# A fifth buffer for retention's values, and the last step of the group norm on ScalarE

## The chip, the cores and the metric

The kernel runs on one core of a Trainium2 chip. A core has a matrix engine (TensorE, PE in the profile; its weight loads are PEld), a vector engine (VectorE, DVE), a scalar engine (ScalarE, ACT), a general engine (GpSimd, POOL) and DMA queues (most of them started by SyncE, SP). The engines run side by side, each takes its own instructions in a fixed order, and they wait for one another through semaphores. The metric is the time of one execution in microseconds on the device.

## The reference, cut to what matters

The kernel computes one layer of a hybrid encoder: 1024 positions and 16 learned meta tokens, width 1024, float32. One projection of the normed input feeds retention (4 heads, keys of 128, values of 256), windowed attention and several gates. The change lies in retention and in the group norm behind it:

```python
    s = jnp.einsum("bnihd,bnjhd->bnhij", q, k) * decay[None, None]
    inner = jnp.einsum("bnhij,bnjhv->bnihv", s, v)
    ...
    kv = jnp.einsum("bnjhd,bnjhv->bnhdv", k * k_decay[None, None, :, :, None], v)
    ...
    cross = jnp.einsum("bnihd,bnhdv->bnihv", q * q_decay[None, None, :, :, None], s_prev)
    return (inner + cross).reshape(B, L, H, DV)
```

This is done forward and backward over blocks of 128 positions and summed. Then each head's 256 values of a position are normed:

```python
    mu = jnp.mean(o_r, axis=-1, keepdims=True)
    var = jnp.mean(jnp.square(o_r - mu), axis=-1, keepdims=True)
    o_r = ((o_r - mu) * lax.rsqrt(var + EPS)).reshape(B, T, RET_V)
```

## The kernel before

Every float32 product is made of three matmuls on halves: a value is split into a high part (a rounded copy) and a low part (the rest), and `mm3` (lines 71 to 76) multiplies high by high, low by high and high by low. The high part is a copy on ScalarE or GpSimd, the low part a subtraction on VectorE (`dve_lo`, line 89).

Retention runs for about the first 340 us, one head after another. The meta tokens are block 0 (16 rows), and the 1024 positions are blocks 1 to 8 of 128 rows. For one head, `retention` does this:

- `stage1(c)` (line 462) projects the values of block c (`projT`, tile `pv`, 24 matmuls of 256 columns; 16 for block 0) into one of the three PSUM banks `pj`. ScalarE copies the high part to `vh` (line 467) and VectorE makes the low part `vl`. For block 0 the values pass through `vmeta` first. Then it transposes the block's keys and multiplies keys and queries (tile `tr`, lines 470 and 472, in one of the two PSUM banks `p1`), scales the keys with the decays (`khf`, `khb` on ScalarE, line 480; low parts on VectorE, line 481) and makes the decayed scores (`sd`, `sh`, `sl`, lines 489 to 491).
- `stage2(c)` (line 502) uses them: the inner and the cross part (`pa`, in the one bank `p3`), which become the output `op` of the block (lines 510 and 511), and the products of keys and values (`pkv`), from which the forward state follows (`Sf`, its halves made by GpSimd and VectorE). The backward products are kept as `kvb` (line 527).
- After all blocks, the loop at line 576 goes backward from block 8 to 1: it updates the backward state, adds its part to the output (`pb`, lines 588 and 589), takes mean and variance of the block (lines 593 and 594), adds the epsilon (line 595, the instruction is kept as `near`) and raises it to the power -0.5 on GpSimd (line 596). The norm itself is kept as a function and run one step later, behind the next block's `near` (lines 600 and 601): a subtraction and a multiplication on VectorE (line 597). Two steps later `finish` transposes the block (tile `to`, line 565, again in `p1`), ScalarE scales it into `ost` (line 570), and SyncE stores it.
- The last two blocks of a head are finished during the next head (`pend`, lines 536 to 538).

In the backward loop, `fill(KT)` offers other work to TensorE: the next head's keys and queries (`gen_qk`), and parts of later stages. For head 3 it is the attention's first projections.

The text's order is not the order on an engine. A planner (`schedule_with_timeline_sim=True`) puts each engine's instructions in order when the kernel is built, by their place in the text and by times that it models itself, and instructions that are ready may overtake others. `tc.issue_after(i)` adds an edge: what is traced under it comes after `i` on `i`'s engine. The order is then fixed. How far a later step can be drawn ahead is limited by buffers: with `bufs=4`, the fifth block's `vh` can be written only when the first block's `vh` has been read for the last time, by `pkv` or `pa` in `stage2`.

Of the kernel before, what the change touches and what calls it, by code (L numbers as in the profile page):

```python
# [7 lines left out]
F32 = mybir.dt.float32  # L8
R = mybir.dt.float32r
AF = mybir.ActivationFunctionType  # L10
ALU = mybir.AluOpType
# [3 lines left out]
NM = 16  # L15
T = NM + SEQ
P = 128
# [21 lines left out]
def block_kernel(ctx: ExitStack, tc: tile.TileContext, xT, x, meta, w_in, w_rb, w_ab, w_out, vecs, dec, sink,  # L39
                 post_w, rope, tab, out):  # L40
    nc = tc.nc
# [29 lines left out]
    def mm3(o, ah, al, bh, bl, first, last, free_group=False):  # L71
        kw = {"skip_group_check": True} if free_group else {}
        nc.tensor.matmul(o, ah, bh, start=first, stop=False, **kw)  # L73
        nc.tensor.matmul(o, al, bh, start=False, stop=False, **kw)  # L74
        latest[:] = [nc.tensor.matmul(o, ah, bl, start=False, stop=last, **kw).ins]  # L75
        return latest[0]
# [11 lines left out]
    def dve_lo(o, i, hi):  # L88
        return nc.vector.tensor_tensor(o, i, hi.bitcast(F32), ALU.subtract).ins  # L89
# [65 lines left out]
    def projT(w, c, name, mt=None):  # L155
        wh, wl = w
        a, b = cols(c)
        t = pj(name)
        if c == 0:
            for k in range(KT):  # L160
                nc.tensor.matmul(t[0:48, 0:256], xm[:, k, 0:48], wh(k, 0, 256), start=k == 0, stop=False,
                                 skip_group_check=True)
                nc.tensor.matmul(t[0:NM, 0:256], xm[:, k, 0:NM], wl(k, 0, 256), start=False, stop=k == KT - 1,
                                 skip_group_check=True)
            nc.scalar.copy(mt, t[32:32 + NM, 0:256])
            nc.vector.tensor_tensor(mt, t[0:NM, 0:256], mt, ALU.add)
            return mt
        for k in range(KT):
            mm3(t[0:b - a, 0:256], xh[k][:, a:b], xl[k][:, a:b], wh(k, 0, 256), wl(k, 0, 256), k == 0, k == KT - 1)
        return t  # L170
# [88 lines left out]
    with tc.tile_pool(name="setup", bufs=1, reuse_waits="tile") as st:  # L259
# [57 lines left out]
        for k in range(KT):  # L317
            t = xr[k]
            parts = [(0, 528), (528, T)] if k == 0 else [(0, T)]
            for a, b in parts:  # L320
                high = nc.scalar.activation(xh[k][:, a:b], t[:, a:b], AF.Copy, scale=vec[:, k:k + 1]).ins
                with tc.issue_after(done) if done is not None and k > 2 else ExitStack():
                    low = nc.vector.scalar_tensor_tensor(xl[k][:, a:b], t[:, a:b], vec[:, k:k + 1],
                                                         xh[k][:, a:b].bitcast(F32), op0=ALU.mult,
                                                         op1=ALU.subtract).ins
# [17 lines left out]
        for c in range(9):  # L343
            a, b = cols(c)
            t = st.tile([P, D if c < 7 else T], F32, tag="xn" if c < 7 else "xr", bufs=7 if c < 7 else KT,
                        name=f"xn{c}")[:, 0:D]
# [46 lines left out]
    def kd_(i, c, n):  # L393
        return kdr[0:n, i, c:c + 1]
# [4 lines left out]
    def qdb(h, c):  # L399
        return qd[:, NH + h, c - 1:c]  # L400
# [4 lines left out]
    def cdb(h):  # L405
        return dtab[:, 24 + h:25 + h]
# [10 lines left out]
    rp = r_stack.enter_context(tc.tile_pool(name="rp", bufs=1, reuse_waits="tile"))  # L417
# [18 lines left out]
    def retention(h, fill):  # L436
# [7 lines left out]
        wv = wv0 if h == 0 else load_w(w_in, U_V + h)  # L444
        kvb = [None] + [rp.tile([P, 256], F32, tag="kvb", bufs=NB - 1, name=f"kvb{h}_{c}") for c in range(1, NB)]
        op = [rp.tile([P, 256], F32, tag="op", bufs=NB, name=f"op{h}_{c}") for c in range(NB)]
        vmeta = rp.tile([NM, 256], F32, tag="vmeta", bufs=2, name=f"vmeta{h}")
        st1 = {}
        state = {"f": None, "b": None}
        pins = []  # L450

        def qs(ts, c):
            return ts[(c - 1) // 4][:, P * ((c - 1) % 4):P * ((c - 1) % 4) + P]

        def ksl(c):
            if c == 0:
                return kt[:, 0, 0:NM]
            i = (c - 1) // 2
            o = P * ((c - 1) % 2) + (NM if i == 0 else 0)
            return kt[:, i, o:o + P]  # L460

        def stage1(c):
            n = NM if c == 0 else P
            pv = first.pop(0) if first else projT(wv, c, f"pv{h}_{c}", vmeta)
            vh = rp.tile([P, 256], R, tag="vh", bufs=4, name=f"vh{h}_{c}")
            vl = rp.tile([P, 256], R, tag="vl", bufs=4, name=f"vl{h}_{c}")
            state["v"] = nc.scalar.copy(vh[0:n], pv[0:n, 0:256]).ins
            state["vl"] = dve_lo(vl[0:n], pv[0:n, 0:256], vh[0:n])
            tr = p1(f"tr{h}_{c}")
            nc.tensor.transpose(tr[0:n, 0:P], ksl(c), ident)  # L470
            if c > 0:
                nc.tensor.matmul(tr[:, P:2 * P], ksl(c), qs(q, c), start=True, stop=True)
            kd = {}
            for d in ("f", "b"):
                if d == "f" and c > 7 or d == "b" and c < 2:
                    continue
                sc = kd_(h, c, n) if d == "f" else kd_(NH + h, c, n)
                a = rp.tile([P, P], R, tag="kh" + d, bufs=2, name=f"kh{d}{h}_{c}")
                b = rp.tile([P, P], R, tag="kl" + d, bufs=2, name=f"kl{d}{h}_{c}")
                nc.scalar.activation(a[0:n], tr[0:n, 0:P], AF.Copy, scale=sc)  # L480
                nc.vector.scalar_tensor_tensor(b[0:n], tr[0:n, 0:P], sc, a[0:n].bitcast(F32), op0=ALU.mult,
                                               op1=ALU.subtract)
                kd[d] = (a, b)
            s = None
            if c > 0:
                sd = rp.tile([P, P], F32, tag="sd", bufs=3, name=f"sd{h}_{c}")
                a = rp.tile([P, P], R, tag="sh", bufs=3, name=f"sh{h}_{c}")
                b = rp.tile([P, P], R, tag="sl", bufs=3, name=f"sl{h}_{c}")
                nc.vector.scalar_tensor_tensor(sd, tr[:, P:2 * P], r2[:, c:c + 1], DT[:, h], op0=ALU.mult, op1=ALU.mult)
                nc.scalar.copy(a, sd)  # L490
                dve_lo(b, sd, a)
                s = (a, b)
            st1[c] = (n, vh, vl, kd, s)

        def split_state(sr_, nm):
            a = rp.tile([P, 256], R, tag="Sh", bufs=2, name=f"Sh{nm}")
            b = rp.tile([P, 256], R, tag="Sl", bufs=2, name=f"Sl{nm}")
            state["S"] = pool_hi(a, sr_)
            dve_lo(b, sr_, a)
            return a, b  # L500
# [60 lines left out]
        def finish(c):  # L561
            o = op[c - 1]
            to = p1(f"to{h}_{c}")
            for e_ in range(2):
                nc.tensor.transpose(to[:, P * e_:P * e_ + P], o[:, P * e_:P * e_ + P], ident)  # L565
            if c % 2 == 0:
                ost[0] = rp.tile([P, 2, 256], F32, tag="ost", bufs=2, name=f"ost{h}_{c}")
            w0 = P * ((c - 1) % 2)
            for e_ in range(2):
                nc.scalar.activation(ost[0][:, e_, w0:w0 + P], to[:, P * e_:P * e_ + P], AF.Copy,  # L570
                                     scale=rnw[:, 2 * h + e_:2 * h + e_ + 1])
            if c % 2 == 1:
                nc.sync.dma_start(
                    oTr_d[2 * h:2 * h + 2, :, P * (c - 1):P * (c + 1)].rearrange("e p t -> p e t"), ost[0])

        for c in range(NB, 0, -1):
            o = op[c - 1]
            if c > 1:
                nxt = kvb[c - 1]
                if c < NB:  # L580
                    nxt = rp.tile([P, 256], F32, tag="S", bufs=2, name=f"Sb{h}_{c}")
                    nc.vector.scalar_tensor_tensor(nxt, state["b"], cdb(h), kvb[c - 1], op0=ALU.mult, op1=ALU.add)
                state["b"] = nxt
                state["bs", c - 1] = split_state(nxt, f"b{h}_{c}")
            if c < NB:
                bh, bl = state["bs", c]
                pb = p3(f"pb{h}_{c}")
                last["pb"] = mm3(pb[:, 0:256], qs(qh, c), qs(ql, c), bh, bl, True, True)
                nc.vector.scalar_tensor_tensor(o, pb[:, 0:256], qdb(h, c), o, op0=ALU.mult, op1=ALU.add)
            bs = rp.tile([P, 6], F32, tag="bs", bufs=2, name=f"bs{h}_{c}")  # L590
            mv = rp.tile([P, 2], F32, tag="mv", bufs=2, name=f"mv{h}_{c}")
            rs = rp.tile([P, 1], F32, tag="rs", bufs=2, name=f"rs{h}_{c}")
            nc.vector.bn_stats(bs, o)
            nc.vector.bn_aggr(mv, bs)
            near = nc.vector.tensor_scalar(rs, mv[:, 1:2], EPS, None, op0=ALU.add).ins
            nc.gpsimd.tensor_tensor(rs, rs, mhalf[:, 0:1], ALU.pow)
            state["n", c] = lambda o=o, mv=mv, rs=rs: nc.vector.tensor_scalar(o, o, mv[:, 0:1], rs, op0=ALU.subtract,
                                                                              op1=ALU.mult)
            if c < NB:
                with tc.issue_after(near):  # L600
                    state["n", c + 1]()
            if c < 8:
                with ExitStack() as behind:
                    for p in pins:
                        behind.enter_context(tc.issue_after(p))
                    fill(KT)
            if c < NB - 1:
                finish(c + 2)
# [958 lines left out]
```

## Time and profile before

| what | value |
|---|---|
| median of three runs | 1073.84 us (1072.59 to 1073.89) |
| profiled execution | 1072.16 us |
| its span (first to last instruction) | 1070.4 us |
| DMA | 179.46 MB, 168 GB/s on average |

The span is shorter than the execution's time, since something lies ahead of the first and behind the last instruction. In the profile's rows, a group has a line, an engine, an operation and the tiles it writes and reads (`out<-in`), its count, its busy time, the mean duration of one, and the idle time of the engine before it with what ended it. Buffer numbers are left out of tile names, so that all blocks' `pv` are one group. A matmul's duration overlaps with that of the next.

### The profile page before, as it was taken

The page shows a single profiled execution, that of the slowest core. Times are in us where ns is not written, and L with a number is a line of the kernel's source. Part 1 is how long each engine was busy: PE and PEld are TensorE (multiplying, and loading weights), DVE is VectorE, ACT ScalarE, POOL GpSimd, SP SyncE. Part 2 cuts the span into 40 slices and gives each one's busy share as a digit, 9 for nine tenths or more (in the row PEclk, how much of TensorE's full clock was granted, in tenths as well). Part 3 has the DMA queues.
Part 4 walks back from the last instruction along what each step waited for, and adds up shares of the span by engine and source line. Part 5 has one row for each costly group of instructions (what it writes and reads, how often), then busy time and mean ns, then how long its engine had stood idle before and what let it go on. Part 6 is the DMA issues. An engine that isn't in the chain of part 4 may idle for free.

```text
span 1070.4 us, 17180 instructions
## 1 busy us (share of the span) xinstructions
PE 1053.5 (98%) x5921; PEld 910.0 (85%) x5921; DVE 872.2 (81%) x1795; ACT 511.1 (48%) x1135; POOL 203.0 (19%) x268
## 2 busy tenths in 40 slices
PE   8999999999999999999999999999999999999997
PEld 7998999989989888988888888887888888787886
DVE  6887778869976887788868988999799799767765
ACT  5531432513413566665577644455456546333432
POOL 2434225143332222232210000000000000110032
PEclk9999999999999999999999999999999999999999
DMA  9321102113121253444357779899934756779363
GB/s 336 158 70 60 60 21 69 61 51 99 50 79 60 70 177 129 129 148 157 131 165 264 250 235 336 267 361 348 363 121 161 239 176 221 237 205 332 112 118 80
DMA packets 89337, 179.46 MB, mean 168 GB/s; under 512 B 9056, under 2 KB 31072, under 8 KB 88432
## 3 DMA queue, kind: packets, MB, share of 16 engines
q1 hardware_dynamic: 85360, 171.77, 47.1%
q0 software_dynamic: 3456, 6.29, 3.9%
q8 instruction: 47, 0.77, 0.3%
q14 instruction: 42, 0.34, 0.1%
q10 hardware_dynamic: 432, 0.28, 0.1%
HBM read 123.78 MB, written 57.67 MB: 170 GB/s over the span
## 4 chain that ended last, share of the span: by engine, by line
PE 85%; DVE 7%; ACT 3%; DMA 2%; issue 2%; SPq 0%; DVEq 0%; POOLq 0%; ACTq 0%
PE bz L74 8%; PE bz L73 8%; PE bz L75 8%; PE pv L75 3%; PE pv L73 3%; PE pv L74 3%; PE br L74 2%; PE br L75 2%; PE br L73 2%; PE bo L74 2%; PE bo L73 2%; PE bo L75 2%; PE ba L74 2%; PE ba L73 2%; PE ba L75 2%
## 5 line engine op out<-in xcount | busy, mean ns | idle before, releaser
L1184 POOL DMA_DIRECT2D mx_d<-c1a x4 | 3.7, 917 | 401.5 <-DVE c1a L1175 401.5
L74 PE MATMUL bz<-T,llz 128*128 128x512 f32 x192 | 75.8, 395 | 0.0
L75 PE MATMUL bz<-T,lhz 128*128 128x512 f32 x192 | 75.6, 395 | 0.0
L73 PE MATMUL bz<-T,lhz 128*128 128x512 f32 x192 | 75.2, 394 | 0.0
L74 PE MATMUL pv<-wh,big 128*128 128x256 f32 x256 | 73.0, 285 | 0.0
L75 PE MATMUL pv<-wl,big 128*128 128x256 f32 x256 | 72.5, 283 | 0.0
L73 PE MATMUL pv<-wh,big 128*128 128x256 f32 x256 | 72.4, 283 | 0.0
L74 PE MATMUL bz<-big,llz 128*128 128x512 f32 x176 | 69.7, 396 | 0.0
L75 PE MATMUL bz<-big,lhz 128*128 128x512 f32 x176 | 69.3, 394 | 0.0
L73 PE MATMUL bz<-big,lhz 128*128 128x512 f32 x176 | 68.9, 394 | 0.0
L1329 ACT ACTIVATE p<-raw,nm 128x401 f32<-128x401 f32 (+1 forms) x64 | 38.4, 602 | 43.5 <-DVE nm L1326 43.4
L74 PE MATMUL paq<-big,wl 128*128 128x512 f32 x128 | 50.8, 397 | 1.0 <-DVE wl L89 1.0
L73 PE MATMUL paq<-big,wh 128*128 128x512 f32 x128 | 51.8, 404 | 0.0
L75 PE MATMUL paq<-big,wh 128*128 128x512 f32 x128 | 50.4, 394 | 0.0
L1339 POOL TENSOR_SCALAR p<-p,den 128x400 f32<-128x400 f32 (+1 forms) x60 | 33.8, 576 | 83.1 <-DVE den L1332 73.7
L75 PEld LDWEIGHTS pv<-wl,big 128*128 128x128 f32 x256 | 48.3, 189 | 0.1
L73 PEld LDWEIGHTS pv<-wh,big 128*128 128x128 f32 x256 | 48.2, 188 | 0.2
L74 PEld LDWEIGHTS pv<-wh,big 128*128 128x128 f32 x256 | 48.2, 188 | 0.0
L74 PEld LDWEIGHTS bz<-T,llz 128*128 128x128 f32 x192 | 36.2, 188 | 8.6 <-DVE llz L89 0.2
L73 PEld LDWEIGHTS bz<-T,lhz 128*128 128x128 f32 x192 | 36.2, 188 | 8.4
L75 PEld LDWEIGHTS bz<-T,lhz 128*128 128x128 f32 x192 | 36.2, 188 | 8.4
L570 ACT ACTIVATE ost<-to,rnw 128x128 f32<-128x128 f32 x64 | 20.1, 365 | 47.7 <-PE to L565 40.5
(622 smaller groups left out, 3631.2 us busy)
## 6 DMA issues: line engine op xcount, KB each, us to landing
wrz<-in_w_in_dram SPq DMA_DIRECT2D x32, 512.0 KB, 6.1
wr<-in_w_in_dram SPq DMA_DIRECT2D x29, 512.0 KB, 3.6
e<-e SPq DMA_DIRECT2D x40, 256.0 KB, 4.0
we<-in_w_in_dram SPq DMA_DIRECT2D x16, 512.0 KB, 3.9
tg<-tg_d SPq DMA_DIRECT2D x32, 256.0 KB, 4.9
T<-preT SPq DMA_DIRECT2D x6, 1024.0 KB, 7.3
xn<-in_x_dram SPq DMA_DIRECT2D x8, 512.0 KB, 8.6
oTr_d<-ost SPq DMA_DIRECT2D x16, 256.0 KB, 2.1
```

Source lines behind the costliest of these rows:

```text
L73: nc.tensor.matmul(o, ah, bh, start=first, stop=False, **kw)
L74: nc.tensor.matmul(o, al, bh, start=False, stop=False, **kw)
L75: latest[:] = [nc.tensor.matmul(o, ah, bl, start=False, stop=last, **kw).ins]
L570: nc.scalar.activation(ost[0][:, e_, w0:w0 + P], to[:, P * e_:P * e_ + P], AF.Copy, scale=rnw[:, 2 * h + e_:2 * h + e_ + 1])
L1184: nc.gpsimd.dma_start(d, to, accum_op=ALU.add)
L1329: last["exp"] = nc.scalar.activation(p[:, 0:1 + wid], raw[e_][:, 0:1 + wid], AF.Exp, scale=-1.0, bias=nm_[:, e_:e_ + 1], accum_out=den[:, ...
L1339: nc.gpsimd.tensor_scalar(pt[e_][:, 0:wid], pt[e_][:, 0:wid], den[:, e_:e_ + 1], 1.0, op0=ALU.mult, op1=ALU.mult)
```

## The change

Three edits are in `retention`. The tiles `vh` and `vl` have five buffers in place of four. `vmeta` has one in place of two. The last step of the norm, (o - mean) rs with rs = (variance + epsilon)^-0.5, is computed as o rs + (-mean rs): VectorE makes the one-column product -mean rs in the place of the mean, and ScalarE applies it as an activation with a scale and a bias column. Both are traced where VectorE's subtraction stood, behind `near`; `issue_after` orders only the VectorE product, as `near` is on VectorE.

```diff
-        vmeta = rp.tile([NM, 256], F32, tag="vmeta", bufs=2, name=f"vmeta{h}")
+        vmeta = rp.tile([NM, 256], F32, tag="vmeta", bufs=1, name=f"vmeta{h}")
...
-            vh = rp.tile([P, 256], R, tag="vh", bufs=4, name=f"vh{h}_{c}")
-            vl = rp.tile([P, 256], R, tag="vl", bufs=4, name=f"vl{h}_{c}")
+            vh = rp.tile([P, 256], R, tag="vh", bufs=5, name=f"vh{h}_{c}")
+            vl = rp.tile([P, 256], R, tag="vl", bufs=5, name=f"vl{h}_{c}")
...
-            state["n", c] = lambda o=o, mv=mv, rs=rs: nc.vector.tensor_scalar(o, o, mv[:, 0:1], rs, op0=ALU.subtract,
-                                                                              op1=ALU.mult)
+
+            def norm(o=o, mv=mv, rs=rs):
+
+                nc.vector.scalar_tensor_tensor(mv[:, 0:1], mv[:, 0:1], -1.0, rs, op0=ALU.mult, op1=ALU.mult)
+                nc.scalar.activation(o, o, AF.Identity, scale=rs, bias=mv[:, 0:1])
+            state["n", c] = norm
```

## The prediction

> **What bounds the kernel now.** I read the page first, then busy time by stage, then the order on TensorE and ScalarE around one head change.
>
> ```profile
> span 1070.4 us, 17180 instructions
> PE 1053.5 (98%) x5921; PEld 910.0 (85%) x5921; DVE 872.2 (81%) x1795; ACT 511.1 (48%) x1135; POOL 203.0 (19%) x268
> PEclk9999999999999999999999999999999999999999
> PE 85%; DVE 7%; ACT 3%; DMA 2%; issue 2%; SPq 0%; DVEq 0%; POOLq 0%; ACTq 0%
> ```
>
> TensorE (PE) is busy for 98% of the span, at full clock, and makes 85% of the chain that ended last. The change leaves its 5921 matmuls as they are. So it can gain only where TensorE stands still or thins out, and lose only where it opens a new hole. The table of windows for retention (about 40 to 340 us) shows where it thins out. Its columns are the window, its length, then busy time and instructions of PE, PEld, DVE, ACT and POOL, clock, DMA share, GB/s.
>
> ```profile
> 40.00:340.00 300.00, 298.20 (x2238) 281.96 (x2238) 244.12 (x617) 99.29 (x296) 103.73 (x145) 1.00 0.18 58
> 95.00:117.00 22.00, 22.00 (x189) 21.84 (x188) 19.12 (x52) 6.04 (x19) 9.66 (x15) 1.00 0.23 76
> 117.00:122.00 5.00, 4.24 (x27) 3.13 (x26) 4.37 (x15) 2.77 (x10) 1.70 (x3) 1.00 0.16 52
> 122.00:127.00 5.00, 5.00 (x43) 4.85 (x42) 3.83 (x13) 2.76 (x10) 1.12 (x2) 1.00 0.17 56
> 187.00:192.00 5.00, 5.00 (x41) 4.59 (x40) 4.76 (x16) 3.04 (x10) 1.59 (x4) 1.00 0.17 56
> 258.00:265.00 7.00, 6.36 (x45) 5.25 (x44) 6.46 (x21) 3.77 (x13) 2.26 (x4) 1.00 0.23 76
> 273.00:283.00 10.00, 9.61 (x78) 9.21 (x77) 9.83 (x28) 4.42 (x17) 3.15 (x4) 1.00 0.32 107
> ```
>
> Matmuls overlap, so a busy PE hides holes; I count instructions. In a dense stretch 189 matmuls take 22 us, 0.1164 us each, or 43 in 5 us. From head 0 to head 1 (117 to 122) only 27 start: 16 short, 1.86 us. From 1 to 2 (187 to 192) 41: 0.23 us. From 2 to 3 (258 to 265) 45 where 60.1 fit: 1.76 us. These three sum to 3.85 us. In 273 to 283, inside head 3, there are 78 where 86 fit: 0.93 us at most, and 0.39 us idle at least; DVE is busy 9.83 of 10 us there.
>
> [...] By matmul busy all retention would have 1.80 us to give; by weight loads the three changes lack 1.87, 0.41 and 1.75 us, 4.03 us. [...]
>
> What opens the hole at 117 us, in TensorE's order (start, duration, instruction):
>
> ```profile
> 117.39 0.38 PE L565 MATMUL to<-ident,op 128*128 128x128 f32 x2
> 117.61 0.27 PE L470 MATMUL tr<-ident,kr 128*16 128x128 f32 x1
> 118.48 0.33 PE L470 MATMUL tr<-ident,kr 128*128 128x128 f32 x1 [0.61 <-ACT ost L570]
> 118.97 0.91 PE L73 MATMUL pkv<-vh,khf 16*128 16x256 f32 x2
> 119.81 0.38 PE L74 MATMUL pkv<-vh,klf 16*128 16x256 f32 x1
> 121.66 0.28 PE L73 MATMUL pv<-wh,big 128*128 128x256 f32 x1
> ```
>
> And ScalarE's copies of the values (`vh`, line 467):
>
> ```profile
> 107.25 0.37 ACT L467 CAST vh<-pv 128x256 fp32r<-128x256 f32 x1
> 120.23 0.37 ACT L467 CAST vh<-pv 128x256 fp32r<-128x256 f32 x1 [0.78 <-PE pkv L74]
> ```
>
> Up to 117 us TensorE fills the backward pass's waits with value products (`pv`) of the next head: block 0 (16 matmuls) and blocks 1 to 6 (24 each). Blocks 0 to 3 are copied into the four `vh`/`vl` buffers, the last at 107.25; 4, 5 and 6 hold the three `pj` banks. Block 4 cannot be copied until block 0 is used, so its copy waits for `pkv` until 120.23, and only then can block 7 have a bank (121.66). Between, TensorE has only the next head's start: transpose, scaled keys on ScalarE and DVE, `pkv`, one waiting on the other.
>
> **The change part by part.** *A fifth `vh`/`vl` pair.* Block 4 can be copied before the head change, its bank goes to block 7, and 24 matmuls, 24 x 0.1164 = 2.79 us, are ready for a hole that lacks 1.86 us (0→1), 0.23 (1→2) and 1.76 (2→3). No engine does more; 2 KB per partition are taken and 1 KB is returned by the second `vmeta` buffer. The single `vmeta` costs nothing: its uses lie a head (about 70 us) apart. Block 7 done early is missing later, between 122 and 131 us, where TensorE then takes the following head's projections; I cost that at nothing because the chain there follows TensorE and not the reverse:
>
> ```profile
> 150.00:160.00 10.00, 5.73 (x10) 1.00 0.01 2
> DVE m_q L182 <- PE pq L75: 4.2, 2, 2.5
> ```
>
> DVE, the fullest engine of the chain, is busy only 5.73 of 10 us in 150 to 160 and waits for projections. If that cover is gone (the chain sets the pace after all), the hole returns at the next change: that is the second case below. I do not take the full 3.85 us, because the planner's order is not the ideal one and the chain's own instructions still have to fall between the 24: 1.6 of 1.86, 0.2 of 0.23, 1.2 of 1.76, together **3.0 us**.
>
> *The norm.* The prices:
>
> ```profile
> L597 DVE TENSOR_SCALAR op<-op,mv,rs 128x256 f32<-128x256 f32 x32 | 13.1, 410 | 0.6 <-POOL rs L596 0.4
> L1229 DVE SCALAR_TENSOR_TENSOR ms<-ms,ms 128x1 f32<-128x1 f32 x9 | 1.4, 157 | 5.3 <-ACT jk L1224 5.3
> L467 ACT CAST vh<-pv 128x256 fp32r<-128x256 f32 x30 | 11.2, 373 | 12.9 <-PE pv L75 8.5 <-PE pkv L74 2.7 <-PE pa L74 1.5
> L510 ACT ACTIVATE op<-pa,rcol 128x256 f32<-128x256 f32 x32 | 15.3, 479 | 50.6 <-PE pa L75 49.9
> L595 DVE TENSOR_SCALAR rs<-mv 128x1 f32<-128x1 f32 x32 | 4.7, 148 | 0.7
> ```
>
> DVE loses 32 x 410 ns and gains 32 x 157 ns (the same kind at one column): 8.1 us less. ScalarE gains 32 activations of 128x256 with a scale and a bias column, a form not in this trace. A plain copy takes 373 ns, one with a scale column 479: 106 per column, so two give 585 ns. The bounds are 479 (the bias is free) and 691 (it costs twice); I take 585, nearest the single-column row. That is 18.7 us on an engine busy 99.29 of 300 us in retention: beside other work. One norm takes 157 + 585 = 742 ns instead of 410: 0.33 us later for the transpose behind it, plus a handover; the bounds are 0.23 and 0.44.
>
> [...]
>
> It is on the path only at a head's end, where `to` follows at once:
>
> ```profile
> 259.58 0.41 DVE L597 TENSOR_SCALAR op<-op,mv,rs 128x256 f32<-128x256 f32 x1
> 260.13 0.41 PE L565 MATMUL to<-ident,op 128*128 128x128 f32 x2
> 116.17 0.40 DVE L597 TENSOR_SCALAR op<-op,mv,rs 128x256 f32<-128x256 f32 x1
> ```
>
> In the change 2→3 the norm ends at 259.99, 0.14 us before its transpose; 0.33 us more is 0.2 us late. In 0→1 it ends at 116.57, 0.82 us before 117.39: nothing. I cost this at 0.4 us (0.2 twice). The 253 ns that DVE is spared per block helps where DVE is full, 273 to 283: of 0.39 to 0.93 us I take 0.2. Below zero: DVE spared at every backward step (about 8 per head) could close holes by itself, but the fifth buffer closes the same ones, so it is not counted twice. What queues behind the new wait: ScalarE runs in order, and behind the norm stand `ost`, `vh` and the next head's `khf`, for which TensorE waits; that is the third case. POOL's part (line 596) and SP's queue are not touched; weights and stores are issued as before.
>
> Sum: 3.0 + 0.2 - 0.4 = **2.8 us** faster. The profiled execution took 1072.16 us (span 1070.4 and 1.76 around it) and would take 1069.4; the median shown, 1073.84, is 1.68 us above it, so I say **1071.0**.
>
> **The rivals.** *The gain is had once* (chance 0.30). If a head's chain, not TensorE's work, sets its length, then block 7 moved forward only makes fillers run out 2.8 us sooner, and holes come back at the next change. For it: DVE is busy 4.37 of 5, 4.76 of 5 and 6.46 of 7 us at the changes. Against: its idling at 150 to 160. About 1 us: 1072.8.
>
> *ScalarE held up by the norm: slower* (0.15). Place: the last two norms of a head, which fall among the next head's first instructions. If the planner puts the norm early, ScalarE stands until POOL's power and DVE's product are there, and `khf` and `vh` wait behind it.
>
> ```profile
> 119.65 0.58 POOL L596 TENSOR_TENSOR rs<-rs,mhalf 128x1 f32<-128x1 f32 x1 [1.39 <-DVE rs L595]
> L480 ACT ACTIVATE khf<-tr,kdr 128x128 fp32r<-128x128 f32 x28 | 10.2, 368 | 8.1 <-PE tr L472 7.8 <-DVE sd L489 0.2
> ```
>
> Price: 0.58 + 0.157 + 0.585 = 1.32 us a norm, two per change, three changes: 7.9 us at most; half of it is 4: 1077.8. It decides once block 7 is already spent before the change (then 2.79 us of cover are missing). Against: ScalarE idles long before most of its groups. [...]
>
> *The fifth buffer isn't used* (0.05): a `pj` bank, not `vh`, limits the lead. Against: the copy at 120.23 waits for `pkv`, not for a bank. About 1073.6.
>
> **How the numbers follow.** Forecast 0.50, rivals 0.30, 0.15 and 0.05. A measurement of this kernel can tell about 0.2%, 2.15 us, from no change (the three runs span 1.3). Faster by more: the forecast and a little of the first rival, 0.52; within: 0.33; slower: 0.15. The low end is all of it: 3.85 + 0.93 = 4.8 us, 1069.0. The high end takes in the two rivals near zero and the mildest of the slower one: 1075.2. Outside lie most of the slower case and little below.
>
> **What would show it.** Right: the copy of block 4 moves to before the head change, and 24 `pv` matmuls stand in the hole; about 42 starts in 5 us at each change; `tr` no longer waits for `ost`; line 597's group becomes 32 ScalarE activations of about 585 ns and 32 DVE products of about 157; DVE's busy time falls by 8 us and ScalarE's rises by 19. Wrong: fillers running out before a change with the counts at 187 and 258 unchanged (first rival); ScalarE idle before the new activation with `khf` late (second). The forecast would also be wrong if the new order moved the later stages: attention has holes of its own,
>
> ```profile
> 340.00:480.00 140.00, 137.08 (x813) 120.01 (x812) 110.02 (x258) 84.53 (x214) 37.34 (x52) 1.00 0.40 129
> ```
>
> 2.92 us of idle TensorE, which a replanned order could enlarge or close.

## The result, and the profile after

The changed kernel takes 1080.07 us (median of six runs, 1077.89 to 1081.83) where the kernel before takes 1073.44 us beside it (1072.44 to 1074.07). The ratio is 1.0061, with a 95% interval of 1.0048 to 1.0074: it is 6.6 us slower, where 2.8 us faster was forecast, with a range of 1069.0 to 1075.2 us. The profiled execution took 1081.83 us; it is the slowest of the six, so the two traces differ by more (9.7 us) than the medians. Three executions among the experiments (one each of the kernel before, of n4_norot and of e8_keep_on) were in a state in which they took 1.6 to 5.5 times as long, and no time given here uses them.

From the page of the changed kernel, the span, the busy times and the chain that ended last:

```profile
span 1080.1 us, 17212 instructions
PE 1056.8 (98%) x5921; PEld 912.2 (84%) x5921; DVE 863.0 (80%) x1795; ACT 527.8 (49%) x1167; POOL 198.3 (18%) x268
PE 73%; DVE 12%; DMA 8%; ACT 3%; issue 3%; SPq 1%; POOL 0%; DVEq 0%; POOLq 0%; ACTq 0%
```

TensorE has the same 5921 matmuls and is busy for the same 98%, in a span that is 9.7 us longer. DVE has lost 9.2 us of work and ScalarE gained 16.7, about as forecast. But TensorE's share of the chain falls from 85% to 73%, and 12 points go to DVE, DMA and issue: somewhere TensorE now waits for others.

The first step of the forecast did happen. ScalarE's copies of the values in the changed kernel (`vh`, start and duration) around the change from head 0 to head 1:

```profile
111.87 0.37 ACT L467 CAST vh<-pv 128x256 fp32r<-128x256 f32 x1
121.59 0.37 ACT L467 CAST vh<-pv 128x256 fp32r<-128x256 f32 x1
```

Block 4 is copied at 111.87 us in place of 120.23, before the head change; it is block 5 that waits now. The windows around the later changes show where the time is lost. First the changed kernel (window, its length, busy time and instructions of PE, PEld, DVE, ACT, POOL, clock, DMA share, GB/s), then the kernel before:

```profile
117.00:122.00 5.00, 5.00 (x43) 4.74 (x41) 2.61 (x9) 2.63 (x8) 1.17 (x2) 1.00 0.17 56
190.00:193.00 3.00, 1.80 (x14) 1.31 (x13) 2.56 (x9) 1.49 (x5) 1.14 (x2) 1.00 0.12 40
193.00:196.00 3.00, 2.69 (x13) 2.35 (x14) 2.30 (x11) 2.47 (x8) 0.95 (x2) 0.67 0.26 87
345.00:350.00 5.00, 2.33 (x11) 1.44 (x10) 2.32 (x8) 1.65 (x4) 0.00 (x0) 1.00 0.46 129
350.00:355.00 5.00, 5.00 (x16) 4.08 (x17) 2.34 (x10) 2.60 (x8) 1.87 (x4) 0.66 0.09 31
```

```profile
190.00:193.00 3.00, 3.00 (x25) 2.87 (x25) 3.00 (x11) 1.83 (x7) 1.12 (x2) 1.00 0.15 50
193.00:196.00 3.00, 3.00 (x28) 3.00 (x27) 1.70 (x6) 1.66 (x6) 0.40 (x1) 1.00 0.02 8
345.00:350.00 5.00, 4.71 (x26) 3.78 (x25) 1.88 (x8) 2.55 (x7) 2.14 (x4) 1.00 0.02 3
350.00:355.00 5.00, 5.00 (x27) 4.17 (x27) 4.58 (x11) 2.43 (x7) 1.14 (x1) 1.00 0.00 0
```

The window from 117 to 122 us holds 43 matmuls in place of 27, as forecast. But the change from head 1 to head 2 (190 to 196 us), which had 53 matmuls, now has 27, and at the entry into attention (345 to 355 us) there are 27 in place of 53. The stages lie up to 5 us later in the changed kernel, but the kernel before has no such window at its own places either: 41 in 5 us at its second change (187 to 192). Behind both holes the granted clock is lower as well: 0.67 and 0.66, which was not foreseen at all.

For all stages, TensorE's lost time was worked out from the records of its matmuls: from one start to the next, less what the same form takes in a dense stretch (0.118 us for 256 columns; 0.235 us was taken for 512 columns, where the trace of the kernel before shows 0.232). Time lost to a halved clock is counted in it. The three kernels e1, e10 and e14 are those of the experiments below.

```
us lost in               before  after    e1    e10    e14
100-130 (head 0 to 1)      2.44   1.94   1.99   1.90   1.99
180-200 (head 1 to 2)      0.60   3.82   2.40   2.26   3.00
250-275 (head 2 to 3)      2.58   2.49   3.07   4.24   3.31
335-365 (into attention)   1.29   6.46   6.42   3.02   2.98
440-500                    3.14   3.87   2.58   2.91   2.77
```

The first change gains 0.5 us where 1.6 was forecast; the second loses 3.2, and the entry 5.2. In the stretches with a granted clock of 0.5 alone, the same working gives 1.6 us for the changed kernel's second change, 1.3 for its entry, 2.6 for the entry in e1 and 1.6 for the third change in e10; the other entries hold none.

### The profile page after: what moved, and what is told of

It reads as the page before. It is cut to its first block, busy times and chain, and to the rows that moved or that the text cites. A ratio compares the mean times of both kernels' runs of the same rounds, so it can differ in the third digit from the quotient of the medians.

```text
span 1080.1 us, 17212 instructions
## 1 busy us (share of the span) xinstructions
PE 1056.8 (98%) x5921; PEld 912.2 (84%) x5921; DVE 863.0 (80%) x1795; ACT 527.8 (49%) x1167; POOL 198.3 (18%) x268
## 4 chain that ended last, share of the span: by engine, by line
PE 73%; DVE 12%; DMA 8%; ACT 3%; issue 3%; SPq 1%; POOL 0%; DVEq 0%; POOLq 0%; ACTq 0%
PE bz L73 3%; PE bz L74 3%; PE bz L75 3%; PE pv L74 3%; PE pv L75 3%; PE pv L73 3%; PE br L74 2%; PE br L73 2%; PE br L75 2%; PE bo L74 2%; PE bo L73 2%; PE bo L75 2%; PE ba L74 2%; PE ba L73 2%; PE ba L75 2%
## 5 line engine op out<-in xcount | busy, mean ns | idle before, releaser
L89 DVE TENSOR_TENSOR wl<-wr,wh 128x1024 fp32r<-128x1024 f32 x28 | 36.0, 1285 | 9.8 <-POOL wh L86 6.2
```

## The experiments

### Each part alone

```diff
 e1_buffers: vh, vl bufs=5, vmeta bufs=1; the norm as before
 e2_norm:    the norm as in the change; vh, vl bufs=4, vmeta bufs=2
 e3_vmeta:   only vmeta bufs=1
```

> The five buffers (and one vmeta) alone, the norm on VectorE as before. Theory A (values drawn ahead leave only key and query projections, with their rotations on VectorE, as fillers of the next head's forward pass, and so slow its chain): 4 to 8 us slower than before, with the forward pass of head 1 some 9 us later at its last block as in the changed kernel. Theory B (the norm's longer way through two engines delays each head's end and the backward pass): within 1.5 us of before, most likely 1 us faster, since the buffers alone can only cover holes.

> The norm on ScalarE alone, four buffers and two vmeta as before. Theory A: within 1.5 us of before. Theory B: 4 to 8 us slower than before, with the last transposes of each head later by 1 us or more against the last backward product, and the entry into attention some 5 us later.

> Only vmeta with one buffer in place of two. Both theories: within 1 us of before, as its uses lie a head apart. If it moved by more than 2 us, the planned order would be so sensitive that a small change of buffers alone explains the size of the result.

Measured against the kernel before (1073.41 us): e1_buffers 1079.7 us, ratio 1.0059 [1.0042, 1.0077]; e2_norm 1076.32, 1.0031 [1.0020, 1.0042]; e3_vmeta 1073.11, 1.0002 [0.9993, 1.0012]. The part that was to gain loses 6.3 us alone; the norm loses 2.9 alone. `vmeta` is nothing, as forecast. e1_buffers lies where theory A put it; e2_norm lies between its two expectations and fits neither. The two losses do not add up: together they are 6.6 us. So the buffers were the question.

### Where on the path the norm is

```diff
 def norm(o=o, mv=mv, rs=rs, c=c):
+    if c > 3:
         nc.vector.scalar_tensor_tensor(mv[:, 0:1], mv[:, 0:1], -1.0, rs, op0=ALU.mult, op1=ALU.mult)
         nc.scalar.activation(o, o, AF.Identity, scale=rs, bias=mv[:, 0:1])
+    else:
+        nc.vector.tensor_scalar(o, o, mv[:, 0:1], rs, op0=ALU.subtract, op1=ALU.mult)
```

This is e6_norm_early on the kernel before; e7_norm_late has `c <= 3` in its place.

> Four buffers; the norm on ScalarE for blocks 8 to 4 of each head and on VectorE for blocks 3 to 1. If the price of the ScalarE norm lies at a head's end (third case of the prediction): within 1 us of before. If it lies anywhere in the backward pass (ScalarE's queue, or the order as a whole): 2 to 4 us slower than before, as e2_norm.

> Four buffers; the norm on ScalarE for blocks 3 to 1 of each head alone. If the price lies at a head's end: 2.5 to 4 us slower than before, as e2_norm (3.3 us). If not: within 1.5 us of before.

e7_norm_late, with the three last blocks of a head on ScalarE, takes 1076.84 us, 1.0031 [1.0020, 1.0043], the whole loss of e2_norm. e6_norm_early, with the five others, takes 1074.49, 1.0013 [1.0002, 1.0023]. Most of the price lies at the head's end, though the two intervals touch. There the changed kernel shows it in TensorE's order and then in ScalarE's:

```profile
192.15 0.44 PE L565 MATMUL to<-ident,op 128*128 128x128 f32 x2 [0.90 <-ACT op L601]
192.43 0.27 PE L470 MATMUL tr<-ident,kr 128*16 128x128 f32 x1
193.31 0.33 PE L470 MATMUL tr<-ident,kr 128*128 128x128 f32 x1 [0.61 <-ACT ost L570]
```

```profile
193.15 0.34 ACT L480 ACTIVATE khf<-tr,kdr 16x128 fp32r<-16x128 f32 x1
193.40 0.58 ACT L601 ACTIVATE op<-op,mv,rs 128x256 f32<-128x256 f32 x1
193.90 0.37 ACT L480 ACTIVATE khf<-tr,kdr 128x128 fp32r<-128x128 f32 x1
194.16 0.59 ACT L601 ACTIVATE op<-op,mv,rs 128x256 f32<-128x256 f32 x1
194.66 0.36 ACT L467 CAST vh<-pv 128x256 fp32r<-128x256 f32 x1
```

`to` waits 0.90 us for the norm, the next head's second transpose behind it waits for `ost`, and two more norms stand between the next head's first `khf` and the `vh` behind it. That is the place that the slower rival named, though its price of up to 1.3 us a norm is not seen here: 0.58 and 0.59 are the activations themselves. The order moved as well: of the eight value matmuls (0.9 us) that stand between head 2's first two `tr` in the kernel before, none stands there in e2_norm, which has four buffers too. How much of the 2.9 us is ScalarE's queue and how much this new order is not separated.

### Are VectorE's fillers the cause of the buffers' loss?

The first theory (A): matmuls drawn ahead bring the next projections into the forward pass sooner, and with them weight splits and rotations on VectorE, which stand in the chain's way; so hold the fillers back (e4_pins5), or take the rotations away (n4_norot against n5_norot).

```diff
 e4_pins5, on e1_buffers:
-            if h == 0 and c == 4:
+            if c == 4:
                 pins.extend((state["v"], state["vl"], state["S"]))
 n4_norot, on the kernel before, and n5_norot, on e1_buffers:
-            rope_evac(t, a, b, kt[:, i], f"k{h}_{i}")
+            nc.scalar.copy(kt[:, i, 0:b - a], t[:, 0:b - a])
...
-            rope_evac(t, a, b, o, f"q{h}_{i}")
+            nc.scalar.copy(o, t)
```

> Five buffers, one vmeta, norm on VectorE, and the fillers of every head (not of head 0 alone) held behind the value copies of block 4 or 5 on their engines. Theory A (the projections drawn forward, with their rotations and weight splits on VectorE, slow the next head's forward pass): head 1's forward pass, from its first key transpose to its last pa, falls from 50.5 us in e1_buffers to 43 us or less (41.8 before), 24 value matmuls stand again in the change from head 1 to 2, and the kernel is 4 us or more faster than e1_buffers (below 1075.7). If the buffers slow it in another way (space, bank use, an order that is bad by chance): within 2 us of e1_buffers.

> The kernel before with the rotation of the next heads' keys and queries left out: gen_qk's projections are copied by ScalarE, and DVE's rotations (m_k, m_q and their sums) of heads 1 to 3 are not made; four buffers, the norm on DVE. It is the base for n5_norot. Theory A (the earlier fillers put DVE's rotations and weight splits into the forward pass's chain) and theory B (the lead itself is harmful, DVE has no part in it) both expect this kernel a little faster than before, 1066 to 1073 us, with head 1's forward pass (first tr to last pa) 36 to 41 us in place of 41.8.

> e1_buffers (five buffers, norm on DVE) with the same rotations left out. Only its difference from n4_norot counts. Theory A: with the rotations gone from DVE most of what five buffers cost goes: n5 minus n4 between -3 and +1 us, and head 1's forward pass within 2 us of n4's (with them it is 50.5 against 41.8, 8.7 longer). Theory B: n5 minus n4 at least +4 us, and head 1's forward pass still 6 us or more longer.

n4_norot and n5_norot leave the rotations out, so they do not compute the layer; only the difference between the two counts. e4_pins5 takes 1082.4 us, 1.0081 [1.0066, 1.0096]: worse, by more than either expectation allowed. The change from head 1 to 2 loses only 1.03 us, but the held fillers leave new holes at 130 to 150 us (1.82 lost, 0.09 in e1_buffers) and at 200 to 220 (3.07, 0.04). n4_norot takes 1071.85 us and n5_norot 1076.85 (0.9991 [0.9981, 1.0001] and 1.0041 [1.0028, 1.0054] of the kernel before): the buffers still cost 5.0 us, and head 1's forward pass is still 5.9 us longer (44.4 against 38.5). So VectorE's rotations are not the cause, or not of more than the 1.3 us between 6.3 and 5.0. The weight splits, which theory A also named, were not taken away. What the two kernels do share with the kernel before and e1_buffers is seen in windows from one head's first `tr` to the next one's, the last ending at attention's first `ps`. The kernel before, then e1_buffers:

```profile
117.60:187.90 70.30, 69.54 (x522) 65.43 (x520) 57.56 (x147) 24.89 (x76) 24.70 (x36) 1.00 0.15 50
187.90:260.40 72.50, 72.40 (x541) 68.33 (x539) 58.01 (x149) 23.72 (x69) 23.48 (x35) 1.00 0.23 74
260.40:342.10 81.70, 80.77 (x595) 75.71 (x594) 64.97 (x173) 30.18 (x88) 25.56 (x35) 1.00 0.18 59
```

```profile
117.50:191.00 73.50, 72.79 (x551) 68.72 (x549) 55.28 (x143) 24.77 (x76) 22.79 (x35) 1.00 0.15 48
191.00:263.80 72.80, 72.26 (x532) 67.80 (x532) 57.12 (x152) 23.46 (x69) 23.68 (x35) 1.00 0.23 73
263.80:345.20 81.40, 78.44 (x570) 72.64 (x568) 64.67 (x169) 30.03 (x87) 23.92 (x35) 1.00 0.18 56
```

In e1_buffers head 1 holds 29 more matmuls and is 3.2 us longer: dense work, with nothing more lost. These matmuls were drawn ahead out of the heads behind. But head 2, with 9 fewer, is 0.3 us longer, and head 3, with 25 fewer, only 0.3 us shorter. The work was moved, its time was paid once, and the two heads that it was taken from are together no shorter. The granted clock is 1.00 in all of these windows, so it has no part in this. The three heads have nearly the same work (1653 recorded matmuls against 1658) and take 3.2 us more. The pair without rotations shows it more weakly, n4_norot and then n5_norot, 3.4 us more for 1662 and 1666 matmuls: heads 2 and 3 are 1.8 us shorter there, for 42 matmuls fewer, which are 4.9 us of work:

```profile
116.80:184.00 67.20, 66.95 (x506) 63.31 (x504) 45.55 (x127) 27.04 (x82) 18.36 (x29) 1.00 0.16 52
184.00:258.80 74.80, 74.80 (x562) 70.83 (x559) 47.70 (x131) 26.01 (x75) 16.81 (x29) 1.00 0.23 72
258.80:340.40 81.60, 80.59 (x594) 75.58 (x592) 64.85 (x173) 30.19 (x88) 25.29 (x35) 1.00 0.18 59
```

```profile
116.30:188.70 72.40, 72.40 (x552) 68.80 (x550) 47.30 (x127) 27.58 (x83) 16.73 (x29) 1.00 0.15 48
188.70:262.50 73.80, 73.24 (x544) 69.00 (x542) 48.21 (x134) 25.77 (x75) 17.87 (x29) 1.00 0.23 72
262.50:343.30 80.80, 78.45 (x570) 72.54 (x568) 64.29 (x169) 29.59 (x87) 23.11 (x35) 1.00 0.18 56
```

### Less lead

```diff
-            vh = rp.tile([P, 256], R, tag="vh", bufs=4, name=f"vh{h}_{c}")
-            vl = rp.tile([P, 256], R, tag="vl", bufs=4, name=f"vl{h}_{c}")
+            vh = rp.tile([P, 256], R, tag="vh", bufs=3, name=f"vh{h}_{c}")
+            vl = rp.tile([P, 256], R, tag="vl", bufs=3, name=f"vl{h}_{c}")
```

(and one `vmeta`, as in the change)

> Three vh/vl buffers and one vmeta, norm on DVE: one block less of lead than before. If less lead is the mirror of more (theory A: lead spent before a head change is given back in the forward pass behind it), head 1's forward pass is as long as before or shorter (39 to 42 us against 41.8), the change 0 to 1 lacks about 2.8 us more than before, and the total is 1073 to 1079 us. If a forward pass is longer by the planner's luck in the order and not by the lead, it can be longer here too (45 us or more).

b3_buffers takes 1078.73 us, 1.0058 [1.0043, 1.0073]. So four buffers stand between two slower neighbours. With three, the loss is at the first change (100 to 130 us: 5.41 us lost against 2.44) and at the second (2.20 against 0.60), while the entry into attention loses less than before (0.97 against 1.29). The 3.0 us more at the first change look like the 24 missing matmuls (2.8), but 1.7 of them lie in a half clock from 120.4 us on. Head 1's forward pass is not shorter, though (43.3 us against 41.8): that part of the mirror fails, and it is not the 45 us or more of the other expectation either.

### The entry into attention

In e1_buffers the order on TensorE at attention's entry has one oddity. TensorE, ScalarE and VectorE there:

```profile
343.65 0.38 PE L565 MATMUL to<-ident,op 128*128 128x128 f32 x2
345.25 0.91 PE L73 MATMUL ps<-kTh,aqh 128*128 128x272 f32 x2 [1.22 <-ACT aqh L633]
347.78 0.60 PE L74 MATMUL ps<-kTh,aql 128*128 128x272 f32 x1 [1.28 <-DVE aql L89]
```

```profile
344.06 0.62 ACT L570 ACTIVATE ost<-to,rnw 128x128 f32<-128x128 f32 x2 [1.83 <-PE to L565]
344.58 1.14 ACT L633 CAST aqh<-aq 128x512 fp32r<-128x512 f32 x2
```

```profile
338.24 0.41 DVE L597 TENSOR_SCALAR op<-op,mv,rs 128x256 f32<-128x256 f32 x1 [0.44 <-POOL rs L596]
...
347.03 0.69 DVE L89 TENSOR_TENSOR aql<-aq,aqh 128x512 fp32r<-128x512 f32 x1 [1.11 <-DMA oTr_d<-ost]
```

Retention's last `to` stands behind nine projections (`paq`, 2.1 us), although its block was normed at 338.65 us (338.24 and 0.41). On ScalarE `aqh` stands behind `ost` (344.58 us behind 344.06); the second `aql` waits, as the trace puts it down, until the store of `ost` has been made; and `ps` waits for both. In the kernel before, `to` stands ahead of the projections:

```profile
339.04 0.38 PE L565 MATMUL to<-ident,op 128*128 128x128 f32 x2
339.99 0.40 PE L73 MATMUL paq<-big,wh 128*128 128x512 f32 x1
342.08 0.41 PE L73 MATMUL ps<-kTh,aqh 128*128 128x272 f32 x2
```

Nobody wrote either order: the planner chose it from the times that it models. An edge that puts `to` first moves two matmuls:

```diff
 e10_to_first, on e1_buffers; e11_after_to_first, on the changed kernel:
-                nc.tensor.transpose(to[:, P * e_:P * e_ + P], o[:, P * e_:P * e_ + P], ident)
+                last["to"] = nc.tensor.transpose(to[:, P * e_:P * e_ + P], o[:, P * e_:P * e_ + P], ident).ins
...
-        with follow(*latest):
+        with follow(*latest, last["to"]):
             fill(3)
```

> e1_buffers (five buffers, norm on DVE) with one edge more: attention's first nine query projections (paq) come behind head 3's last transpose (to of block 1) on TensorE. In e1_buffers that transpose stands behind them (343.65 us, the ps behind it waits 1.22 us for ScalarE and 1.28 for DVE, and the clock is halved for 6.8 us); in the kernel before it stands ahead of them, and the edge would change nothing there. Theory C (most of what five buffers cost is this one place): the entry into attention (335 to 365 us) loses 1 to 2.5 us in place of 6.4, no half clock there, total 1074 to 1076 us. Theory D (the cost is spread over the longer forward passes, and the entry only shows a delay that is owed anyway): 1078 us or more, the loss appearing further on.

> The whole change with the same edge. Theory C: 4 to 5 us less than the changed kernel (1080.07), 1075 to 1076.5 us, with the change 1 to 2 (180 to 200 us, 3.8 us lost) left as it is. Theory D: 1079 us or more.

e10_to_first takes 1077.44 us, 1.0035 [1.0023, 1.0048], and e11_after_to_first 1077.86, 1.0039 [1.0026, 1.0052]: 2.3 and 2.2 us less than without the edge, by medians. In the trace of e10_to_first the projections now cover the wait for `aqh`, while the one for the second `aql` stays (1.33 us):

```profile
343.10 0.38 PE L565 MATMUL to<-ident,op 128*128 128x128 f32 x2
345.41 0.41 PE L73 MATMUL ps<-kTh,aqh 128*128 128x272 f32 x2
```

From `ps` to the first of the matmuls `bz` behind attention are 225.4 us before, 228.8 in e1_buffers and 226.5 in e10_to_first; 2.6 of the 228.8 are the half clock, which e10_to_first does not have there. So the entry is real and about a third of the loss (2.3 of 6.3), in part by way of the clock. Both kernels fall between the theories: theory C, that the entry is most of it, expected more; theory D, that it only shows a delay owed anyway, gave 1078 and 1079 us or more, near the upper ends of the two intervals (1078.5 and 1078.9). From head 0's first `tr` to `ps` are 307.6 us in e10_to_first, against 307.9 in e1_buffers and 304.2 before. About 1.6 us of the 307.6 are a half clock at 267 us (granted 0.91 over 255 to 275 us) in this one execution; without it, 1.8 us of the 3.7 would be left. With the edge, then, head 3 does become shorter, by part of what was taken from it. In e11_after_to_first, at full clock, it takes 80.1 us, 1.6 less than before, for 25 matmuls fewer (2.9 us):

```profile
265.40:345.50 80.10, 78.13 (x570) 72.70 (x568) 60.13 (x168) 34.90 (x97) 23.63 (x34) 1.00 0.19 57
```

### The clock

```diff
 e8_keep_on and e9_keep_on2 (the same kernel), on e1_buffers, ahead of attention's first scores:
+            keep_on = pj("keep_on")
+            for _ in range(12):
+                latest[:] = [nc.tensor.matmul(keep_on, xh[0][:, NM:NM + P], xh[1][:, NM:NM + 512], start=True,
+                                              stop=True).ins]
```

> e1_buffers with 12 extra matmuls of 512 columns (their result is not used) between the last transposes of retention and attention's first scores, where TensorE stood for 2.5 us with the clock at 0.65 afterwards. If the halved clock after the hole is worth what its record says (6.8 us at half speed in e1_buffers, 3.4 us lost): the clock stays at 1.00 through 340 to 360 us and the kernel is 1.5 to 3 us faster than e1_buffers although it does 2.8 us more of matmuls. If the clock follows from something else than the hole: 0 to 3 us slower than e1_buffers.

> The same kernel as e8_keep_on, once more for its trace: five buffers, and twelve matmuls of 512 columns on data that nobody uses ahead of attention's first scores. If the half clock at 346 us in e1_buffers follows from TensorE's holes just before it, the granted clock stays 1.00 in 335 to 365 us here. If it has another cause, it drops there all the same. Time about 1079.5 us as measured for it; if the clock is held and the time still is that of e1_buffers, the clock was not what cost.

e8_keep_on has the times: 1079.24 us, 1.0052 [1.0033, 1.0070]; e9_keep_on2 has the trace, of its one run of 1077.29 us. e1_buffers and then e9_keep_on2:

```profile
345.00:350.00 5.00, 3.34 (x11) 2.75 (x12) 2.56 (x7) 1.95 (x6) 0.00 (x0) 0.65 0.54 157
```

```profile
345.00:350.00 5.00, 4.49 (x23) 3.56 (x22) 3.02 (x10) 2.11 (x7) 0.00 (x0) 1.00 0.52 157
```

With the hole filled by work that nobody needs (12 x 0.232 = 2.8 us), the clock stays at 1.00 from 335 to 365 us, as was expected if the half clock follows from the hole. One execution of each kernel does not prove it, since the clock falls at other places in other traces. From `ps` to `bz` e9_keep_on2 takes 225.3 us, as the kernel before: the 3.4 us that e1_buffers loses there are the half clock (2.6) and a longer wait for `aql` (1.28 in place of 0.51). What it costs in the whole is not settled by the times, which lie within e1_buffers' own range (1078.45 to 1081.23) but for the one traced run, and which hold 2.8 us of work more.

### What the prediction took the fifth buffer to do

```diff
 e14_hold_tr, on e10_to_first:
+            with follow(last["tr"]) if h and c == 7 else ExitStack():
                 pv = first.pop(0) if first else projT(wv, c, f"pv{h}_{c}", vmeta)
...
-            nc.tensor.transpose(tr[0:n, 0:P], ksl(c), ident)
+            t0 = nc.tensor.transpose(tr[0:n, 0:P], ksl(c), ident).ins
+            if c == 0:
+                last["tr"] = t0
```

> e10_to_first with block 7's value products of heads 1 to 3 held behind the first transpose of their own head, so that 24 matmuls stand in each head change between tr of block 0 and tr of block 1, which is what the prediction took the fifth buffer to do. If the change's holes only lack matmuls there: the changes 1 to 2 and 2 to 3 lose under 1 us each (2.4 and 3.1 in e1_buffers), total 1071 to 1073 us, at or under the kernel before. If the chain of a head sets its length (the stock of matmuls is used up ahead of the change all the same): the hole moves to the last steps of the backward pass, and the total stays within 1 us of e10_to_first.

e14_hold_tr takes 1077.92 us, 1.0039 [1.0025, 1.0054], within 0.5 us of e10_to_first. The 24 matmuls stand in every head change, and the hole is elsewhere. At the end of head 1's backward pass, e10_to_first and then e14_hold_tr:

```profile
185.00:190.00 5.00, 5.00 (x45) 5.00 (x44) 2.67 (x8) 1.25 (x4) 0.98 (x2) 1.00 0.17 56
```

```profile
185.00:190.00 5.00, 3.58 (x29) 3.02 (x27) 4.21 (x14) 1.72 (x6) 2.18 (x4) 1.00 0.16 52
```

45 matmuls become 29, just ahead of the change that is now filled: 16 x 0.1164 = 1.9 us, and the change's own hole had been 2.26. The granted clock is 1.00 here from 37 to 365 us (0.999 over the whole execution), so this kernel's loss is not the clock's. By this the stock of matmuls that do not wait for the chain is what is short, not their place.

## Why the prediction was wrong

- **Four buffers limit the lead, and a fifth lets block 7 forward: right.** The copy moved from 120.23 to 111.87 us, and 43 matmuls stand between 117 and 122 us. `vmeta` costs nothing: right (1.0002).
- **1.6 us from the first change: too much.** The hole went from 2.44 to 1.99 us lost in e1_buffers. Of the 24 matmuls that were to stand in each change, 20, 0 and 0 stand between the first two `tr` of heads 1, 2 and 3 there (11, 0 and 0 in the changed kernel, 0, 8 and 0 before). They push the next head's own first steps back: the last matmul of head 1's first `pa` starts at 126.5 us in e1_buffers, at 125.1 before.
- **"Block 7 done early is missing later ... I cost that at nothing because the chain there follows TensorE and not the reverse": this step failed.** It holds in head 1, which became longer by just the 29 matmuls it took on. It does not hold for the heads that they came from: heads 2 and 3 have 34 matmuls fewer, 4.0 us of work, and are together as long as before. The first rival had the mechanism ("fillers run out sooner, and holes come back at the next change"), but gave it a small gain; it is a loss, since the stock is gone before the second change (2.40 us lost in place of 0.60) and before the third (3.07 in place of 2.58). 0.2 and 1.2 us had been forecast as gains there. The prediction read DVE's idle time at 150 to 160 us as proof for all heads: one stretch of head 1 said nothing of heads 2 and 3.
- **The later stages were left out of the sum.** The text named a replanned order at attention's entry as what could make it wrong and gave it no price and no rival. It lost 5.1 us in e1_buffers, 2.6 of them at half clock; the place of one transpose is worth about 2.3 in the whole time.
- **The norm: the prices were right, the path was not.** 599 ns for the activation and 150 for the product were forecast at 585 and 157:

```profile
L601 ACT ACTIVATE op<-op,mv,rs 128x256 f32<-128x256 f32 x32 | 19.2, 599 | 20.4 <-DVE mv L600 20.4
```

  But "0.4 us (0.2 twice)" for the late `to` was the only cost put down for a half that lost 2.9 us alone. The term counted the delay of one transpose, and not what stands behind it on ScalarE (`ost`, and the first `khf` and `vh` of the next head, at a place where TensorE has little else), nor that the order changes with it. e7_norm_late and e6_norm_early show the place; the parts of the price are read from one trace only. The second rival named that place and let it decide only once "block 7 is already spent before the change"; e2_norm, with four buffers, shows that it needs no such condition.
- **The granted clock was taken to stay at 1.00.** In the traced execution of the changed kernel it was halved twice while matmuls ran, for 3.41 us each, which accounts for 2.9 us.
- **The third rival's 1073.6 us does not follow from its terms.** Without the 3.0 us the prediction's own sum leaves 0.4 - 0.2 = 0.2 us slower, 1074.0.

Left open: which instruction sets the length of heads 2 and 3 when they have fewer matmuls (the rotations do not), and how much of the median's loss comes from the clock, whose mean over an execution went from 0.995 to 0.998 in the six runs of the changed kernel. It is also not shown that five buffers lose under every order: each kernel was measured with the one order that the planner chose for it, and no run holds the order fixed while the buffers change. No version was found that beats the kernel before.

## What to carry to other kernels

Work that is drawn ahead is a stock, and a larger buffer fills it once; it gains at the next hole only if the chain behind it gets shorter by what was taken out (here heads 2 and 3 of e1_buffers, with 34 matmuls fewer, were no shorter), so compare instruction counts and lengths of whole periods (one head's first transpose to the next one's), not the one hole. Where a planner sets the order, an edit can move distant instructions too: look first at the stages that the edit does not touch, for an instruction that is ready but stands behind others. A longer step on an idle engine is priced by what queues behind it at the place where the bound engine has nothing else, not by that engine's busy share (here 599 ns on an engine busy for 49% in the changed kernel, and 2.9 us lost in e2_norm).

## What the runs showed of the hardware

The clock was halved behind stretches in which TensorE was far from idle (busy for 56 to 78% in the four below). The stretches are 3.4 us long, about as long as each of the two drops in the changed kernel (3.41 us). In e1_buffers it fell at 346.5 us for 6.83 us, and in the 3.4 us ahead TensorE was busy for 60%:

```profile
343.10:346.50 3.40, 2.04 (x10) 1.18 (x8) 0.97 (x4) 1.65 (x4) 0.00 (x0) 1.00 0.26 80
346.50:349.90 3.40, 2.12 (x7) 1.98 (x8) 1.77 (x6) 1.23 (x4) 0.00 (x0) 0.51 0.53 152
```

In the changed kernel it fell at 194.0 and 351.1 us, for 3.41 us each, behind 3.4 us that were busy for 56% and 57%:

```profile
190.60:194.00 3.40, 1.89 (x13) 1.28 (x12) 2.66 (x12) 2.48 (x8) 1.69 (x3) 1.00 0.00 0
347.70:351.10 3.40, 1.95 (x10) 1.36 (x9) 1.92 (x6) 0.82 (x4) 0.00 (x0) 0.99 0.78 229
```

The kernel before has a hole at the first head change that left TensorE busy for 2.65 of 3.40 us (78%), and no half clock there:

```profile
116.80:120.20 3.40, 2.65 (x17) 1.81 (x15) 2.58 (x9) 1.40 (x5) 1.35 (x3) 1.00 0.23 77
```

The busy share alone does not decide, though. In e10_to_first the clock fell at 267.07 us behind 3.41 us that were busy for 78% as well, and in e14_hold_tr it did not fall behind 3.4 us that were busy for 58%:

```profile
263.66:267.07 3.41, 2.65 (x17) 1.78 (x16) 2.91 (x10) 1.54 (x5) 1.20 (x2) 1.00 0.31 103
```

```profile
186.40:189.80 3.40, 1.98 (x14) 1.44 (x13) 3.17 (x13) 1.25 (x4) 1.64 (x3) 1.00 0.23 77
```

What sets off a drop is therefore not settled here.

Single waits were short. In the 3.4 us ahead of the drops in the changed kernel and in e1_buffers the longest one of TensorE was 1.32 us (`ps` for `aql` in the changed kernel), and in e7_norm_late TensorE stood still for 1.41 us in all from 340 to 350 us, where the clock fell too (0.66 from 345 to 350 us). No single long hole stood ahead of these drops.
